# Leaving the softmax weights of eight heads unnormalised until the output projection loads them

## The chip, the cores and the metric

The kernel runs on one core of a Trainium2 chip, float32 in and out. The metric is the device time of one execution in microseconds (us), the median of several. PE is the matrix engine, PEld its weight loads, DVE the vector engine, ACT the scalar engine, POOL GpSimd, SP the engine whose queue issues all DMAs of this kernel.

## The reference, cut

Two layers of an encoder with 1024 tokens of width 1024. Each layer projects the normalised input, runs four groups of four heads, projects their 1024 concatenated outputs with `w_out`, adds a residual, and ends in a gated MLP. The groups are A (2-D neighbourhood), B (low-rank, "latent"), C (grouped-query) and D (sliding window). Only B and C are touched; both are dense attention:

```python
sc = jnp.einsum('bqhgd,bkhd->bhgqk', q_blk, k).astype(jnp.float32) * scale
p = jax.nn.softmax(sc, axis=-1).astype(v.dtype)
return jnp.einsum('bhgqk,bkhd->bqhgd', p, v)
...
mixed = jnp.concatenate([o_a, o_b, o_c, o_d], axis=-1) @ w_out[l]   # shapes left out
```

## The kernel before

Every fp32 matmul is made of rounded halves: an operand is split into a high part (a cast to the rounded type, on ACT or DVE) and a low part (the difference, on DVE or POOL).

Per layer the mixer runs sixteen heads in the order d0 to d3, c0 to c3, b0 to b3, a0 to a3, and of each head four pairs of 128-query tiles; one pair is a slot. `score` (L1030) works a slot: two score tiles of 128x1024 for a head of c or b (L1028), the negated row maximum on DVE (L1086), the exponential on ACT with the row sum as a by-product (L1105), the reciprocal of the sum on DVE (L1129), and for c and b the multiplication of the whole 128x1024 tile `P` by it on DVE (L1131). `gather` (L1142) then transposes the weights in chunks of four 128x128 blocks (L1183), casts the high half from PSUM on ACT (`PTh`, L1188), subtracts for the low half on DVE (`PTl`, L1193), multiplies both with the values on PE into `ob_mix` (L1210), adds the two halves of the result (`bot`, L1245) and stores it to DRAM in `oT` (L1249), transposed: 64 rows of a head by 1024 tokens. `PTh` and `PTl` take turns in a ring of five buffers (tag `PT`, `NPT` = 5).

The output projection runs a group behind, in the gaps: `out_group` (L771) loads two heads' rows of `oT` for half of the tokens at a time (L800, into a free part of `bias`), casts the high half on DVE (L801), makes the low half on POOL (L802), multiplies by `w_out` on PE (`pb_mix`, `od`, `oc`, `ob` with `wod`, `woc`, `wob`) and adds into `y` on DVE (L828). Group d is projected while c and b run, c while b and a run, b while a runs.

Each step is put at a time by a table `P` of numbers; a scheduler then orders every engine's instructions from those, their operands and the free buffers. Each engine and the SP queue work their instructions in that order, and an instruction that waits holds all behind it. Group a also loads many small pieces through SP: `va` (L895) and `za` (L865, L870).

Of the kernel before, what the change touches and what calls it, by code (L numbers as in the profile page):

```python
# [10 lines left out]
F32 = mybir.dt.float32  # L11
F32R = mybir.dt.float32r
AF = mybir.ActivationFunctionType
ALU = mybir.AluOpType
# [5 lines left out]
S = 1024  # L20
# [24 lines left out]
def r32(ap):  # L45
    return ap.bitcast(F32)
# [25 lines left out]
NP, NPT = 6, 5  # L72


class Kernel:
# [16 lines left out]
    def setup(self):  # L92
        nc, tc, ctx = self.nc, self.tc, self.ctx
        cp = self.cp = ctx.enter_context(tc.tile_pool(name="const", bufs=1))
        dr = self.dr = ctx.enter_context(tc.tile_pool(name="dram", bufs=1, space=DRAM))
        self.wp = ctx.enter_context(tc.tile_pool(name="wp", bufs=1))
        self.sm = ctx.enter_context(tc.tile_pool(name="small", bufs=8))
        self.big = ctx.enter_context(tc.tile_pool(name="big", bufs=1))
        self.psp = None
        self.banks_for("mix0")  # L100

        self.mhalf = cp.tile([128, 1], F32, name="mhalf", tag="mhalf")
        nc.vector.memset(self.mhalf, -0.5)
        self.eps = cp.tile([128, 1], F32, name="eps", tag="eps")
        nc.vector.memset(self.eps, EPS)
        self.z = dr.tile([NPIECE, 128, NT, 128], F32, name="z", tag="z")
        self.oT = dr.tile([D, S], F32, name="oT", tag="oT")
        self.gate = dr.tile([NFF, 128, S], F32, name="gate", tag="gate")
        self.xs = [dr.tile([S, D], F32, name=f"xs{i}", tag=f"xs{i}") for i in range(2 * DEPTH - 1)]


        self.gcol = cp.tile([128, DEPTH, NK], F32, name="gcol", tag="gcol")
        self.idf = cp.tile([128, 128], F32, name="idf", tag="idf")
        self.idr = cp.tile([128, 128], F32R, name="idr", tag="idr")
# [655 lines left out]
    def out_group(self, l, kind):  # L770

        nc = self.nc
        ov = self.oT.rearrange("(g k p) s -> g p k s", p=128, k=2)
        g = "abcd".index(kind)
        tag = f"{kind}{l}"
        ws = {}

        def begin():
            assert all(self.ow.get((kind, i)) == 4 for i in range(2 if kind == "a" else 4))
            if kind == "d":  # L780
                self.y = [self.share(i, F32, f"y{l}_{i}", (4, S)) for i in range(2)]
            if kind == "a":

                ws["x"] = [[self.reg["K"][:, e, :] for e in range(2)], self.o1]
            else:
                if kind == "d":
                    self.o = self.share(2, F32R, f"o{l}", (2, 2, S))
                ws["x"] = [(self.o[:, k, 0], self.o[:, k, 1]) for k in range(2)]

        def load(c):  # L790

            if c == 0:
                begin()
            assert kind in "ad" or all(("bcd"["bcd".index(kind) + 1], "mm", 4 * c + t) in self.ow for t in range(4))
            cols = slice(c * 512, c * 512 + 512)
            for k, (hi, lo) in enumerate(ws["x"]):
                if kind == "a" and k == 1:
                    break
                raw = self.bias[:, 3, (c if kind == "a" else k) * 512:][:, :512]
                nc.sync.dma_start(raw, ov[g, :, k, cols])  # L800
                nc.vector.tensor_copy(hi[:, cols], raw)  # L801
                nc.gpsimd.tensor_tensor(out=lo[:, cols], in0=raw, in1=r32(hi[:, cols]), op=ALU.subtract)  # L802

        def raw():
            ws["raw"] = [self.raw_weights([self.w_out[l][:, i * 512:(i + 1) * 512]], 2 * g, 2, f"wo{tag}_{i}")
                         for i in range(2)]

        def split():
            ws["w"] = [self.split_weights(x, f"wo{tag}_{i}") for i, x in enumerate(ws["raw"])]

        def mm(t, i):
            self.ow[kind, "mm", t] = 1
            bank = None if i else "pb"
            ws["ps", t, i] = ps = self.ps1([128, 512], F32, f"o{tag}") if bank is None else self.half(bank, True)
            if kind == "a":
                assert self.ow[kind, 2] == 4 and (kind, 3, t // 4 * 2 + 1) in self.ow
            with self.begin(bank):
                last = self.mm3(ps, [([x[:, t * 128:(t + 1) * 128] for x in ws["x"][k]], [x[:, k, :] for x in ws["w"][i]])
                                     for k in range(2)])
            self.through(bank, last)  # L820

        def add(t, i):
            ps = ws["ps", t, i]
            y = self.y[t // 4][:, t % 4, i * 512:(i + 1) * 512]
            if kind == "d":
                nc.scalar.copy(y, ps)
            else:
                nc.vector.tensor_tensor(out=y, in0=y, in1=ps, op=ALU.add)  # L828

        return dict(load=load, raw=raw, split=split, mm=mm, add=add)  # L830

    def slot(self, kind, n):
# [198 lines left out]

    def score(self, hd, pair, t0, ln):

        nc, kind, i = self.nc, hd["kind"], hd["i"]
        st = hd[pair] = dict(P={})
        tag = f"{hd['tag']}_{pair}"

        def tile(j, t):
            qt = 2 * pair + j
            x = {}  # L1040
# [5 lines left out]
            else:  # L1046

                r0, e = 8 * (pair // 2) + 4 * j, pair % 2
# [62 lines left out]
            def norm():  # L1111
                st["ok"] = j + 1
                if kind in "da" and j == 0:
                    return
                rr = st["rr"][:, j:j + 1]
                if kind == "d":

                    nc.vector.tensor_tensor(out=st["sum"], in0=st["sum"], in1=st["es"], op=ALU.add)
                    nc.vector.reciprocal(st["rr"], st["sum"])
                    if st["pd"][0].shape == x["p"].shape:  # L1120
                        both = st["p"].rearrange("p (a b) -> p a b", b=512)[:, :, :n]
                        todo = [(both, st["rr"].unsqueeze(2).to_broadcast([128, 2, n]))]
                    else:
                        todo = [(p, st["rr"][:, e:e + 1].to_broadcast(list(p.shape))) for e, p in st["pd"].items()]
                elif kind == "a":
                    nc.vector.reciprocal(st["rr"], st["sum"])
                    todo = [(p, st["rr"][:, e:e + 1].to_broadcast(list(p.shape))) for e, p in st["pd"].items()]
                else:
                    nc.vector.reciprocal(rr, st["sum"][:, j:j + 1])  # L1129
                if kind in "bc":  # L1130
                    nc.vector.tensor_scalar(out=x["p"], in0=x["p"], scalar1=rr, scalar2=None, op0=ALU.mult)  # L1131
                    return
                for p, r in todo:
                    nc.gpsimd.tensor_tensor(out=p, in0=p, in1=r, op=ALU.mult)
# [3 lines left out]
            self.at(t + d, top)  # L1138
            self.at(t + d + n / 1000 + P["EXP"], exp)
            self.at(t + d + n / 500 + P["EXP"] + P["NRM"], norm)  # L1140

        tile(0, t0 + P[f"S{kind.upper()}0"] * ln)  # L1142
# [666 lines left out]
```

## Time and profile before

| | us |
|---|---|
| median of three runs | 2690.39 (2689.8 to 2691.87) |
| the profiled execution, its own time | 2694.25 |
| its span, first to last instruction | 2692.4 |
| PE busy in the span | 2565.2 |
| DVE busy | 2111.1 |
| ACT busy | 1463.6 |

The first layer's heads of c and b lie at about 290 to 558 us of the span, its heads of a at 558 to 640, and what turns `y` into the MLP's operands up to 720. The second layer repeats this from 1622. Idle time of an engine is put to what released it; a releaser written `DVE P_b L1131` is the last DVE instruction of that line before the wait ended. PE's ends are modelled, so a busy PE can still stand between two matmuls; its waits show better on PEld, which must load the weights first.

### The profile page before, as it was taken

How to read it: one execution, taken by the hardware profiler on the slowest of the kernel's cores; microseconds unless marked ns; L12 is line 12 of the kernel's file. 1: busy time of each engine (PE TensorE's matmuls, PEld its weight loads, DVE VectorE, ACT ScalarE, POOL GpSimd, SP SyncE). 2: the span in 40 equal slices, each digit the busy share in tenths (PEclk: the TensorE clock that was granted, in tenths of full speed). 3: DMA queues.
4: the chain of work that ended last, by engine and by line, in shares of the span. 5: the costliest groups of instructions: out<-in, count | busy, mean ns of one | idle time of the engine just before them, and what ended most of it. 6: DMA issues, size and time to landing. Idle time of an engine off the chain costs nothing. (4 is left out here: it accounts for less than half of the span.)

```text
span 2692.4 us, 40234 instructions
## 1 busy us (share of the span) xinstructions
PE 2565.2 (95%) x14533; PEld 2210.0 (82%) x14533; DVE 2111.1 (78%) x3099; ACT 1463.6 (54%) x2704; POOL 798.2 (30%) x761
## 2 busy tenths in 40 slices
PE   7999999997799999999999999999968999999998
PEld 7999888885688888788789998888757888888886
DVE  5347899989878888878854568999797778888787
ACT  5347677666544444544653466776664444454433
POOL 1343212264333343100234432112743333330001
PEclk9999999999899999999999999999988999999999
DMA  6343412234222222550352434122432222226502
GB/s 190 106 131 91 107 49 68 56 72 152 76 90 77 94 79 79 188 203 17 97 163 86 124 96 94 50 71 55 113 126 79 71 95 71 86 71 227 179 1 102
DMA packets 316913, 268.00 MB, mean 100 GB/s; under 512 B 104762, under 2 KB 262570, under 8 KB 316714
## 3 DMA queue, kind: packets, MB, share of 16 engines
q1 hardware_dynamic: 316714, 265.43, 32.9%
q8 instruction: 114, 1.87, 0.3%
q14 instruction: 85, 0.70, 0.1%
HBM read 183.30 MB, written 69.48 MB: 94 GB/s over the span
## 5 line engine op out<-in xcount | busy, mean ns | idle before, releaser
L1309 POOL TENSOR_TENSOR sums<-loads 128x512 f32<-128x512 f32 x84 | 170.0, 2023 | 153.0 <-DMA loads<-in_w_up 67.2
L1309 POOL TENSOR_TENSOR loads<-loads,sums 128x512 f32<-128x512 f32 x42 | 57.7, 1374 | 372.4 <-DVE wgl L1319 229.5
L1530 ACT CAST dhP<-rows 128x1024 fp32r<-128x1024 f32 x88 | 89.4, 1052 | 130.1 <-issue 53.7
L86 POOL TENSOR_TENSOR rs_pf<-rs_pf,mhalf 128x1 f32<-128x1 f32 x15 | 13.9, 928 | 467.7 <-ACT rs_pf L85 467.6
L1531 DVE TENSOR_TENSOR dlP<-rows,dhP 128x1024 fp32r<-128x1024 f32 x88 | 105.2, 1219 | 40.7 <-ACT dhP L1530 40.7
L255 PE MATMUL dx<-dhP 128*128 128x512 f32 x308 | 120.2, 390 | 1.1 <-DVE yfQ L1597 1.1
L257 PE MATMUL dx<-dhP,dlP 128*128 128x512 f32 x308 | 120.0, 389 | 0.0
L256 PE MATMUL dx<-dlP,dhP 128*128 128x512 f32 x308 | 119.8, 389 | 0.0
L1188 ACT CAST PTh_b<-pt_b 128x512 fp32r<-128x512 f32 x128 | 74.9, 587 | 57.6 <-PE pt_b L1183 56.5
L257 PE MATMUL ux<-fT,wql 128*128 128x512 f32 (+1 forms) x272 | 102.6, 377 | 0.0
L255 PE MATMUL pb_mix<-whi_wa,h 128*128 128x256 f32 x320 | 100.0, 313 | 0.1
L1376 ACT ACTIVATE c<-ug,cw 128x1024 f32<-128x1024 f32 x44 | 54.7, 1244 | 82.4 <-DMA gate<-c 79.4
L255 PE MATMUL ux<-fT,wqh 128*128 128x512 f32 (+1 forms) x256 | 96.9, 378 | 1.4 <-ACT fT L275 1.4
L1377 DVE SCALAR_TENSOR_TENSOR c<-ug,cw,c 128x1023 f32<-128x1023 f32 x44 | 56.8, 1291 | 51.4 <-ACT c L1376 51.4
L256 PE MATMUL ux<-fT,wqh 128*128 128x512 f32 (+1 forms) x256 | 96.5, 377 | 0.0
L1419 ACT ACTIVATE c<-c 128x1024 f32<-128x1024 f32 x44 | 46.7, 1062 | 85.7 <-DVE c L1379 85.7
L1193 DVE TENSOR_TENSOR PTl_c<-pt_c,PTh_c 128x512 fp32r<-128x512 f32 x128 | 85.5, 682 | 8.5 <-ACT PTh_c L1188 7.9
L1188 ACT CAST PTh_c<-pt_c 128x512 fp32r<-128x512 f32 x128 | 74.5, 587 | 32.4 <-PE pt_c L1183 30.6
L1193 DVE TENSOR_TENSOR PTl_b<-pt_b,PTh_b 128x512 fp32r<-128x512 f32 x128 | 87.0, 683 | 6.3 <-ACT PTh_b L1188 5.4
L1028 PE MATMUL s_b<-rK,rQ 128*128 128x512 f32 x256 | 91.5, 414 | 0.4 <-ACT P_b L1105 0.4
L257 PE MATMUL pb_mix<-whi_wa,h 128*128 128x256 f32 x320 | 90.3, 282 | 0.0
L256 PE MATMUL pb_mix<-wlo_wa,h 128*128 128x256 f32 x320 | 90.3, 282 | 0.0
(681 smaller groups left out, 9710.5 us busy)
## 6 DMA issues: line engine op xcount, KB each, us to landing
loads<-in_w_up SPq DMA_DIRECT2D x84, 512.0 KB
gate<-c SPq DMA_DIRECT2D x44, 512.0 KB
z<-z SPq DMA_DIRECT2D x28, 512.0 KB
rows<-gate SPq DMA_DIRECT2D x56, 256.0 KB
rows<-in_w_down SPq DMA_DIRECT2D x56, 256.0 KB
rK<-rK SPq DMA_DIRECT2D x48, 256.0 KB
xs<-xo SPq DMA_DIRECT2D x16, 512.0 KB
xf<-xs SPq DMA_DIRECT2D x16, 512.0 KB
```

The lines of the kernel that those rows point to most:

```text
L255: nc.tensor.matmul(out, ah, bh, start=start and i == 0, stop=False, **flags)
L256: nc.tensor.matmul(out, ah, bl, start=False, stop=False, **flags)
L257: last = nc.tensor.matmul(out, al, bh, start=False, stop=stop and i == n - 1, **flags)
L1028: nc.tensor.matmul(out[:, c:c + w], Q[:, qt * 128:(qt + 1) * 128], K[:, k0 + c:k0 + c + w], start=i == 0, stop=i == len(ops) - 1)
L1188: nc.scalar.copy(x["sp"][0][:np, :n], x["pt"][:np, :n])
L1193: nc.vector.tensor_tensor(out=x["sp"][1][:np, :n], in0=x["pt"][:np, :n], in1=r32(x["sp"][0][:np, :n]), op=ALU.subtract)
L1309: nc.gpsimd.tensor_tensor(out=out, in0=a, in1=b, op=op)
L1376: nc.scalar.activation(c, u, AF.Identity, bias=b, scale=w1)
L1377: nc.vector.scalar_tensor_tensor(out=c[:, 1:], in0=u[:, :S - 1], scalar=w0, in1=c[:, 1:], op0=ALU.mult, op1=ALU.add)
L1419: nc.scalar.activation(a, a, AF.Gelu_apprx_tanh)
L1530: nc.scalar.copy(hi, src)
L1531: nc.vector.tensor_tensor(out=lo, in0=src, in1=r32(hi), op=ALU.subtract)
```

## The change

The 128 multiplications of L1131 go. After the second tile of a slot the two reciprocals of each of 128 rows, `rr`, are stored by one DMA to a new DRAM tile `rsum` of 8 heads by 1024 tokens. When `out_group` loads rows of b or c, it takes a further buffer `r` from the ring `PT`, fills it with two DMAs (for each of two heads one row of 512 sums, repeated over 64 partitions), and multiplies the raw rows by it on DVE before the split. The transposes now take the weights as the exponential leaves them.

```diff
+        self.rsum = dr.tile([8, S], F32, name="rsum", tag="rsum")
...
                 nc.sync.dma_start(raw, ov[g, :, k, cols])
+                if kind in "bc":
+                    r = self.ap.tile([128, 512], F32, tag="PT", name=f"r{tag}_{c}_{k}", bufs=NPT)
+                    for e in range(2):
+                        nc.sync.dma_start(r[64 * e:64 * e + 64], self.rsum["bc".index(kind) * 4 + 2 * k + e, cols]
+                                          .partition_broadcast(64))
+                    nc.vector.tensor_tensor(out=raw, in0=raw, in1=r, op=ALU.mult)
                 nc.vector.tensor_copy(hi[:, cols], raw)
...
                 if kind in "bc":
-                    nc.vector.tensor_scalar(out=x["p"], in0=x["p"], scalar1=rr, scalar2=None, op0=ALU.mult)
+                    if j == 1:
+                        nc.sync.dma_start(self.rsum["bc".index(kind) * 4 + i, pair * 256:pair * 256 + 256]
+                                          .rearrange("(j p) -> p j", p=128), st["rr"])
                     return
```

The scheduler orders the engines anew. In the changed program the lines below L802 are 7 to 10 higher. On DVE, where group c's last slot (`c0_3_3`: layer 0, head 3, pair 3) meets b's first, before:

```order
L1129 RECIPROCAL rr_b0_0_0_5431<-sum_b0_0_0_5429 128x1
L801 CAST o0_4176<-bias0_4172 128x512
L1131 TENSOR_SCALAR P_b0_0_0_0_5433<-P_b0_0_0_0_5433,rr_b0_0_0_5431 128x1024
L1193 TENSOR_TENSOR PTl_c0_3_3_2_5483<-pt_c0_3_3_2_5477,PTh_c0_3_3_2_5482 128x512
L1129 RECIPROCAL rr_b0_0_0_5431<-sum_b0_0_0_5429 128x1
L1131 TENSOR_SCALAR P_b0_0_0_1_5461<-P_b0_0_0_1_5461,rr_b0_0_0_5431 128x1024
L1193 TENSOR_TENSOR PTl_c0_3_3_3_5510<-pt_c0_3_3_3_5504,PTh_c0_3_3_3_5509 128x512
L1086 TENSOR_REDUCE nm_b0_0_1_5533<-s_b0_0_1_0_5537 128x1
L1193 TENSOR_TENSOR PTl_b0_0_0_0_5531<-pt_b0_0_0_0_5525,PTh_b0_0_0_0_5530 128x512
```

and after, on the same engine at the same place:

```order
L1137 RECIPROCAL rr_b0_0_0_5416<-sum_b0_0_0_5414 128x1
L1203 TENSOR_TENSOR PTl_c0_3_3_2_5468<-pt_c0_3_3_2_5462,PTh_c0_3_3_2_5467 128x512
L1137 RECIPROCAL rr_b0_0_0_5416<-sum_b0_0_0_5414 128x1
L1203 TENSOR_TENSOR PTl_c0_3_3_3_5494<-pt_c0_3_3_3_5488,PTh_c0_3_3_3_5493 128x512
L1203 TENSOR_TENSOR PTl_b0_0_0_0_5515<-pt_b0_0_0_0_5509,PTh_b0_0_0_0_5514 128x512
L1094 TENSOR_REDUCE nm_b0_0_1_5517<-s_b0_0_1_0_5521 128x1
```

The two multiplications are gone, and the cast of `o` that stood between has moved to a later place, behind its new product.

On the SP queue, where group b's second half of rows is loaded during the heads of a (`va0_2` are pieces of head a2's values, `oT<-bot` result stores), before:

```order
L1249 DMA oT_81<-bot_a0_0_2_7580 64x8x32
L895 DMA va0_2_7629<-z_80 40x2x64 x23
L1249 DMA oT_81<-bot_a0_0_3_7678 64x8x32
L800 DMA bias0_4172<-oT_81 128x512
L1249 DMA oT_81<-bot_a0_1_0_7760 64x8x32
```

and after:

```order
L1259 DMA oT_81<-bot_a0_0_2_7573 64x8x32
L902 DMA va0_2_7622<-z_80 40x2x64 x24
L1259 DMA oT_81<-bot_a0_0_3_7671 64x8x32
L801 DMA bias0_4169<-oT_81 128x512
L805 DMA rb0_1_0_7701<-rsum_82 64x512 x2
L801 DMA bias0_4169<-oT_81 128x512
L805 DMA rb0_1_1_7708<-rsum_82 64x512 x2
L1259 DMA oT_81<-bot_a0_1_0_7761 64x8x32
```

The four loads of sums stand behind the 24 small loads, and the second raw load stands here too.

On DVE, around the first low half of the second pair of head a1 (`PTl_a0_1_1_0`), before:

```order
L1193 TENSOR_TENSOR PTl_a0_1_0_1_7699<-pt_a0_1_0_1_7694,PTh_a0_1_0_1_7698 120x384
L1126 RECIPROCAL rr_a0_1_2_7657<-sum_a0_1_2_7655 128x2
L1096 ISA P_a0_1_3_0_7748,nm_a0_1_3_7743<-s_a0_1_3_0_7747,bi0_1_7378 128x440
L1096 ISA nm_a0_1_3_7743 128x1
L1193 TENSOR_TENSOR PTl_a0_1_1_0_7742<-pt_a0_1_1_0_7736,PTh_a0_1_1_0_7741 120x512
L1245 TENSOR_TENSOR bot_a0_1_0_7760<-ob_mix0_73,bot_a0_1_0_7760 64x256
```

and after:

```order
L1104 ISA P_a0_2_2_0_7990,nm_a0_2_2_7985<-s_a0_2_2_0_7989,bi0_2_7720 128x440
L1104 ISA nm_a0_2_2_7985 128x1
L1104 ISA P_a0_2_2_0_7990,nm_a0_2_2_7985<-s_a0_2_2_0_7989,bias0_4169 128x320
L1104 ISA nm_a0_2_2_7985 128x1
L807 TENSOR_TENSOR bias0_4169<-bias0_4169,rb0_1_0_7701 128x512
L1203 TENSOR_TENSOR PTl_a0_1_1_0_7743<-pt_a0_1_1_0_7737,PTh_a0_1_1_0_7742 120x512
L808 CAST o0_4173<-bias0_4169 128x512
```

The chunk of head a1 now stands behind the product with the sums, and behind the score bias of head a2's pairs 0 to 2, which the kernel before had later.

## Rows read from the trace of the kernel before

**Rows 1.** The page's first part: busy time, share of the span, instructions.

```profile
PE 2565.2 (95%) x14533; PEld 2210.0 (82%) x14533; DVE 2111.1 (78%) x3099; ACT 1463.6 (54%) x2704; POOL 798.2 (30%) x761
```

**Rows 2.** Busy time by stage: window, its length, each engine, PE clock, DMA.

```profile
core 0: us, PE busy (x) PEld busy (x) DVE busy (x) ACT busy (x) POOL busy (x), PEclk, DMA share, GB/s
290.00:558.00 268.00, 264.25 (x1766) 230.23 (x1766) 248.51 (x432) 195.99 (x369) 60.39 (x61) 1.00 0.27 65
558.00:640.00 82.00, 75.79 (x462) 63.12 (x463) 68.70 (x158) 50.77 (x121) 50.77 (x68) 1.00 0.39 104
640.00:720.00 80.00, 56.89 (x353) 47.99 (x352) 71.24 (x93) 43.95 (x87) 20.91 (x21) 0.87 0.31 106
1622.00:1892.00 270.00, 265.53 (x1773) 231.16 (x1773) 250.23 (x435) 197.21 (x371) 60.91 (x61) 1.00 0.27 65
```

**Rows 3.** Instruction groups on DVE: line, shapes, count | busy us, mean ns | idle before.

```profile
L1131 DVE TENSOR_SCALAR P_c<-P_c,rr_c 128x1024 f32<-128x1024 f32 x64 | 52.1, 816 | 0.5
L1131 DVE TENSOR_SCALAR P_b<-P_b,rr_b 128x1024 f32<-128x1024 f32 x64 | 50.8, 793 | 0.7
...
L757 DVE TENSOR_TENSOR y<-y 128x512 f32<-128x512 f32 x32 | 20.4, 683 | 0.0
...
L1434 DVE TENSOR_TENSOR c<-c,c 128x1024 f32<-128x1024 f32 x44 | 85.6, 1946 | 1.1
```

**Rows 4.** Waits of PEld, 290 to 560 us: us in total, times, longest.

```profile
PEld ob_mix L1210 <- DVE PTl_b L1193: 2.2, 5, 1.2
PEld pt_c L1183 <- ACT rQ L1001: 1.8, 6, 0.4
PEld pt_b L1183 <- DVE P_b L1131: 1.7, 3, 1.3
PEld ob_mix L1210 <- DVE PTl_c L1193: 1.1, 3, 0.7
PEld pt_c L1183 <- DVE P_c L1131: 1.1, 2, 0.9
PEld pt_b L1183 <- ACT rK L1001: 1.0, 4, 0.3
```

**Rows 5.** Line 1131 in the whole execution: who waited for it.

```profile
  PEld pt_b L1183: 3.4, 6
  PEld pt_c L1183: 2.3, 4
```

**Rows 6.** Waits of ACT, 290 to 560 us, for the row maxima.

```profile
ACT P_b L1105 <- DVE nm_b L1086: 4.3, 8, 1.5
...
ACT P_c L1105 <- DVE nm_c L1086: 2.3, 5, 0.6
```

**Rows 7.** SP's issues by line: ns min/median/max of one; then its longest waits, 290 to 700.

```profile
L1249 SPq DMA_DIRECT2D oT<-bot_b x32: 445/468/613, 429.7 to 1896.4; - x32
L931 SPq DMA_DIRECT2D rK<-rK x24: 579/596/646, 187.6 to 1924.8; - x24
SPq L1249 <- DVE bot_c L1245: 46.9, 10, 8.0
SPq L1249 <- DVE bot_b L1245: 27.0, 10, 7.8
```

**Rows 8.** Timeline, start and us: a raw load's issue on SP, its cast on DVE.

```profile
280.97 0.34 SPq L800 DMA_DIRECT2D bias<-oT  x1
283.75 0.43 DVE L801 CAST o<-bias 128x512 fp32r<-128x512 f32 x1 [1.89 <-DMA bias<-oT]
```

**Rows 9.** Timeline of SP, then of DVE, during the heads of a.

```profile
573.31 0.62 SPq L1249 DMA_DIRECT2D oT<-bot_a  x1
573.99 9.13 SPq L895 DMA_DIRECT2D va<-z  x23
583.23 0.62 SPq L1249 DMA_DIRECT2D oT<-bot_a  x1
583.90 0.63 SPq L800 DMA_DIRECT2D bias<-oT  x1
...
580.40 0.69 DVE L1193 TENSOR_TENSOR PTl_a<-pt_a,PTh_a 120x512 fp32r<-120x512 f32 x1
```

## The prediction

> **What bounds the kernel now.** The page's first part says PE is busy 95% of the span, DVE 78% [rows 1], so the question is how far PE stands still where the change acts. The view by stage answers for the heads of c and b: of 268 us PE is busy 264.25 and DVE 248.51, that is 98.6% and 93% [rows 2]. The second layer is alike: 265.53 and 250.23 of 270. PE bounds this stage, and DVE is so full that PE often meets an operand that DVE has not finished. How much that costs is in the waits of PEld, the view to trust where PE's ends are modelled [rows 4]: the waits of 290 to 560 us add up to some 17 us, none longer than 1.3. I sort them by what PE waited for. For the normalised weights: 1.7 and 1.1, together 2.8. For the low halves that DVE makes: 2.2 and 1.1 and three smaller ones of 1.2 together, in all 4.5. For copies and exponentials of ACT: 1.8, 1.0 and nine smaller ones of 4.5 together, in all 7.3. After 558 us the picture turns: in the heads of a PE is busy 75.79 of 82 and DVE 68.70, and then, to 720 us, PE only 56.89 of 80 and DVE 71.24, at a granted PE clock of 0.87 [rows 2]. There DVE is close to the bound.
>
> **The change part by part.**
>
> *The removed multiplications.* DVE loses 52.1 + 50.8 = 102.9 us [rows 3], all inside the stages of c and b. This is off the path: PE is the engine that ends the stage. What the span can gain is PE's waits.
>
> (1) Transposes wait for the exponential instead of the product. The waits for L1131 vanish: 2.8 us in layer 0, and 3.4 + 2.3 = 5.7 in both layers [rows 5].
>
> (2) DVE's queue gets shorter. In layer 0 its work falls from 248.5 to about 248.5 - 51.4 + 2.7 = 200 us, 75% of 268 (51.4 is half of 102.9; 2.7 is (4), below). A low half then waits less behind other DVE work. The waits in question are 0.2 to 1.2 us, the product that stood ahead of them takes 0.8 [rows 3, 4]. So I take half of 4.5, 2.25 us a layer; bounds 0 and 4.5.
>
> (3) ACT waits 4.3 + 2.3 = 6.6 us for row maxima that DVE is late with [rows 6], and the copies behind those exponentials are among what PE waits for. I take a third of 7.3, 2.4 us a layer; bounds 0 and 7.3.
>
> Together 2.8 + 2.25 + 2.4 = 7.45 a layer, 15 us in both. What is late next is PE itself.
>
> *The added products.* (4) Per layer 8 products of 128x512, 16 in all. The nearest row is another sum of two SBUF operands of that shape, 683 ns [rows 3]: 10.9 us of DVE. The four of group c fall to the heads of b, where DVE has just lost far more: nothing, with that slack as cover. The four of group b fall to the heads of a, with DVE at 84% and nearly full after: I charge them in full, 4 x 0.683 = 2.7 a layer, 5.4 us in both. Bounds: 0, if DVE's 13 idle us of that stage take them, and a stretched product. For that the rows give 1946 ns for 1024 elements [rows 3], 973 for 512, so 7.8 us. The Trainium skill ("SBUF", section "Who interferes with whom") says that a DVE instruction with two SBUF inputs contends with a GpSimd instruction that reads SBUF; the stage of a is where POOL is busiest, 50.77 of 82 us [rows 2], so by this rule the term is nearer 7.8, by the short row 5.4. I stay with 683 ns since both kinds of row exist and half of POOL's work there is short.
>
> *The stores of sums.* (5) 32 DMAs a layer of 128x2 values. No row shows 256 runs of four bytes. The nearest issues take 0.47 us (64 runs) and 0.6 (64 runs of an on-chip copy) [rows 7]: 15 to 19 us of SP a layer, 0 if SP only waits then. In that stage SP waits 46.9 + 27.0 us for `bot` alone [rows 7], so I take 0. Behind each store on SP stand result stores, swaps of K and loads of z; it waits for the reciprocal of its own slot, which comes before the result that the next store waits for anyway. The cover is that wait; without it 19 us of SP a layer would come before the K that PE needs. The store also keeps `rr` longer, but the next writer of that buffer comes two slots later, about 17 us.
>
> (6) *The loads of sums.* Eight DMAs a layer and group, 0.596 us each by the nearest row [rows 7]: 4.8 us of SP. For c they stand among waits: 0. A load needs about 2.8 us from issue to use (280.97 to 283.75, a whole 256 KB) [rows 8]. In the new DVE order the first product of c stands six instructions behind the reciprocal that frees the queue for them, some 4.3 us of work, so I take no wait there; bound 2.8 a layer. For b they stand behind 24 small loads; I take 0, bound 4.8 a layer of SP's time in a stage in which SP works almost without a gap [rows 9]. The worse course is rival C.
>
> (7) *The ring.* `r` holds two of five `PT` buffers for some 3 to 5 us, four times a layer. A chunk takes two buffers, so one and a half chunks stay in flight. I take 0 because the order puts other matmuls there; the cost without that cover is one wait of about 2.8 us each, 11 a layer, the upper end of C.
>
> The sum: -15 + 5.4 = -9.6 us. Against the profiled execution that is 2694.25 - 9.6 = 2684.7 (its span 2692.4 to 2682.8); the median of the runs lies 3.9 us under that execution, so the forecast is 2690.4 - 9.6 = **2681 us**. Its own range, with (2) to (4) at milder values, is 2673 to 2688.
>
> **The rivals.**
>
> *A, DVE was the brake of the whole stage.* If all of PE's waits for DVE and ACT vanish, the gain is 2 x (2.8 + 4.5 + 7.3) = 29.2, and 29.2 - 5.4 = 23.8 remain: 2667. For it: DVE at 93%. Against it: ACT is busy only 196 of 268 us, so many of its late copies come from the fixed order rather than from DVE.
>
> *B, hidden anyway.* Only the direct waits go, 5.7, and the products cost 5.4: 2690. For it: PE is busy 98.6% of the stage, and each wait removed can reappear at the next in-order operand, which in the new order is the exponential on ACT.
>
> *C, the small transfers stall the heads of a.* On SP the loads of sums stand behind 24 loads that take 9.13 us for 23, 0.4 each though they move 20 KB each [rows 9]. In the trace they end at 583.12; two result and raw issues follow to 584.53, then two loads of sums of 0.6 (584.5 to 585.7), the second landing 2.8 after its issue began, at 587.9, and the product, 588.6. The low half of head a1 that stands behind this product ran at 580.40 [rows 9]. That is 8.2 us a layer, 16.4 in both: 2690.4 - 15 + 5.4 + 16.4 = 2697, slower. It decides once DVE reaches the product before 587.9. Against it: the new order gives DVE, between the result of head a0's third pair and the product, eleven score biases, three low halves, six additions and more, some 16 us, whereas SP needs about 15. That is close. The Trainium skill ("DMA: Bandwidth & Descriptors", section "Rules for kernel authors") speaks against the change here: it says to coalesce many small transfers, as one under 64 KB is mostly overhead. The trace agrees, with 0.4 us of queue for 20 KB [rows 9] and 0.34 for 256 KB [rows 8].
>
> **How the numbers follow.** Forecast 0.44, A 0.14, B 0.22, C 0.20. The likeliest gives 2681. The range is 2660 to 2700: below it is A with free products (2661), above it C with the ring's waits. About 0.2% (5.4 us) is what a measurement of this kernel can tell from no change. Faster by more than that is under 2685: A and most of the forecast, 0.55. Within: B and the forecast's upper edge, 0.25. Slower, over 2695.8: C, 0.20.
>
> **What would show it.** In the changed profile no transposes wait for a DVE multiplication; DVE is busy about 200 us of the stage of c and b; PEld's waits for low halves halve, and those for ACT shrink by a third; the stage shortens by 5 to 9 us a layer. The heads of a and what follows to the MLP take as long as before, plus up to 3. C would show as DVE or PEld waiting for a DMA `rb<-rsum` or its product, B as new waits of transposes for the exponential. The forecast is wrong if the stage of c and b keeps its 268 us, or if more than 3 us a layer come back between 558 and 720.

## The result

| | before | after |
|---|---|---|
| median of the runs (us) | 2691.13 (2689.8 to 2692.05) | 2819.51 (2816.09 to 2823.49) |
| ratio, 95% interval | | 1.0478 (1.046 to 1.0496) |
| the profiled execution, its span | 2694.25, 2692.4 | 2818.06, 2816.1 |

The change costs 128.4 us, where 10 were forecast as a gain. The page of the changed kernel answers to [rows 1], its windows to [rows 2]:

```profile
span 2816.1 us, 40448 instructions
...
PE 2612.5 (93%) x14533; PEld 2242.1 (80%) x14533; DVE 2052.5 (73%) x2987; ACT 1467.0 (52%) x2704; POOL 794.0 (28%) x761
```

```profile
290.00:558.00 268.00, 234.77 (x1481) 204.03 (x1481) 176.85 (x302) 165.40 (x304) 41.62 (x36) 0.93 0.41 57
558.00:640.00 82.00, 71.98 (x443) 60.39 (x441) 60.84 (x124) 47.56 (x101) 34.39 (x55) 0.96 0.35 66
...
1622.00:1892.00 270.00, 242.66 (x1667) 218.07 (x1666) 181.92 (x370) 173.85 (x359) 57.85 (x51) 0.94 0.48 73
```

In the same 268 us PE does 1481 matmuls instead of 1766, stands still for 33 us instead of 4, and its granted clock falls from 1.00, the upper of its two levels (2.4 GHz; the lower is 1.2), to a mean of 0.93. Over the whole execution PE is busy 47 us longer for the same 14533 matmuls ([rows 1]); how much of the loss is this slower work behind the stalls, and how much the stalls themselves, no run separates. DVE has become idle, as wanted, and nobody profits. The DMA engines are busier, 0.41 for 0.27, and move less, 57 GB/s for 65: the first sign of the cause.

How late each group of heads ends in layer 0 shows in the issues of the result stores of b and of the first two heads of a (ns min/median/max of one, first and last start), of before, then of after:

```profile
L1249 SPq DMA_DIRECT2D oT<-bot_b x16: 445/468/613, 429.7 to 562.5; - x16
L1249 SPq DMA_DIRECT2D oT<-bot_a x8: 580/620/625, 565.8 to 601.9; - x8
```

```profile
L1259 SPq DMA_DIRECT2D oT<-bot_b x16: 445/478/1907, 445.9 to 609.5; - x16
L1259 SPq DMA_DIRECT2D oT<-bot_a x8: 615/620/636, 615.2 to 665.9; - x8
```

Group b ends 47 us late and these heads of a 64 us late. The second layer repeats it: there the last of these stores of a is issued at 2059.7 us instead of 1935.8, 124 us late.

What PEld, DVE and SP wait for in the changed kernel, 290 to 640 us (in total, times, longest), is of a new kind. In [rows 4] no wait exceeds 1.3 us:

```profile
PEld ob_mix L1220 <- DVE bot_b L1255: 17.6, 4, 7.2
PEld pb_mix L256 <- DVE o L808: 8.1, 2, 8.0
PEld ob_mix L1220 <- DVE PTl_c L1203: 6.7, 3, 6.3
PEld s_c L1035 <- issue: 4.5, 1, 4.5
...
DVE bias L807 <- DMA rc<-rsum: 17.0, 3, 8.3
...
ACT bot_b L1240 <- DMA oT<-bot_b: 10.6, 2, 8.6
ACT P_a L1113 <- DMA rsum<-rr_b: 7.4, 1, 7.4
...
PE s_c L1035 <- DMA rK<-rK: 4.3, 1, 4.3
...
SPq L902 <- DMA rsum<-rr_b: 18.3, 4, 5.7
...
SPq L801 <- DMA oT<-bot_d: 10.8, 1, 10.8
```

These are a few long stalls. Eight stops of PEld are longer than 2 us, and the seven of them over 3 us can be followed back to a DMA that landed late: one to the raw load of group d, three to loads of sums (`rc<-rsum`), one to a swap of K, one to a result store that still held its buffer `bot_b`, and one to a store of sums, for which an exponential of a waited 7.4 us. One in full, on SP's timeline of the changed kernel (start, us), then on DVE and PEld:

```profile
291.79 0.38 SPq L1140 DMA_DIRECT2D rsum<-rr_c  x1
292.21 0.47 SPq L1021 DMA_DIRECT2D bias<-rpb  x1
292.78 0.45 SPq L1259 DMA_DIRECT2D oT<-bot_d  x1
293.33 0.53 SPq L342 DMA_DIRECT2D z<-sta  x1
293.95 0.44 SPq L850 DMA_DIRECT2D z<-z  x1
305.23 0.33 SPq L801 DMA_DIRECT2D bias<-oT  x1
...
307.94 0.43 DVE L808 CAST o<-bias 128x512 fp32r<-128x512 f32 x1 [8.02 <-DMA bias<-oT]
...
309.02 0.50 PEld L1220 LDWEIGHTS ob_mix<-PTl_c,rV 128*128 128x128 f32 x2 [6.26 <-DVE PTl_c L1203]
```

Before, the same two steps follow each other at once:

```profile
292.72 0.45 SPq L1249 DMA_DIRECT2D oT<-bot_d  x1
293.27 0.53 SPq L341 DMA_DIRECT2D z<-sta  x1
293.90 0.44 SPq L843 DMA_DIRECT2D z<-z  x1
294.67 0.33 SPq L800 DMA_DIRECT2D bias<-oT  x1
```

The raw load must wait until the result store has landed. Before, the raw load follows 2 us after the issue of that store; behind a store of sums it follows after 12. DVE stands 8 us at the cast, the low half behind the cast is late, and PE behind that. The store of sums itself took SP only 0.38 us.

### The profile page after: what moved, and what is told of

Same layout as the page of the kernel before. It is cut to its first block, busy times and chain, and to the rows that moved or that the text cites. A ratio compares the mean times of both kernels' runs of the same rounds, so it can differ in the third digit from the quotient of the medians.

```text
span 2816.1 us, 40448 instructions
## 1 busy us (share of the span) xinstructions
PE 2612.5 (93%) x14533; PEld 2242.1 (80%) x14533; DVE 2052.5 (73%) x2987; ACT 1467.0 (52%) x2704; POOL 794.0 (28%) x761
## 5 line engine op out<-in xcount | busy, mean ns | idle before, releaser
L256 PE MATMUL pb_mix<-whi_wa,h 128*128 128x256 f32 x320 | 101.1, 316 | 0.1
L1035 PE MATMUL s_c<-rK,rQ 128*128 128x512 f32 x256 | 83.4, 430 | 10.8 <-DMA rK<-rK 10.8
L1094 DVE TENSOR_REDUCE nm_c<-s_c 128x1 f32<-128x1024 f32 x64 | 77.8, 1216 | 21.2 <-PE s_c L1035 21.0
L1113 ACT ACTIVATE P_c<-s_c,nm_c 128x1024 f32<-128x1024 f32 x64 | 71.7, 1121 | 38.5 <-DVE nm_c L1094 38.4
```

The source lines that it names most:

```text
L256: nc.tensor.matmul(out, ah, bh, start=start and i == 0, stop=False, **flags)
L1035: nc.tensor.matmul(out[:, c:c + w], Q[:, qt * 128:(qt + 1) * 128], K[:, k0 + c:k0 + c + w], start=i == 0, stop=i == len(ops) - 1)
L1094: nc.vector.tensor_reduce(nm, x["s"], axis=AX.X, op=ALU.max, negate=True)
L1113: nc.scalar.activation(x["p"], x["s"] if kind in "bc" else x["p"], AF.Exp, bias=st["nm"][:, j:j + 1], scale=1.0 if kind in "bc" else -1.0, ...
```

## The experiments

Each difference below is to the kernel before, run beside it (medians 2687.9 to 2691.1). By the intervals of the ratios each is known to some 3 to 5 us.

| what is in the kernel | us | to before |
|---|---|---|
| normalisation gone, nothing added | 2689.19 | -1.8 |
| ... and products | 2695.17 | +5.5 |
| ... and loads into the ring | 2719.64 | +28.7 |
| ... and stores: the change | 2819.51 | +128.4 |
| before, with the stores | 2754.84 | +63.9 |

The first theory held that the stores cost it all (S), its rivals the loads (L) or the new rhythm without the normalisation (N).

**Stores alone.** In the kernel before:

```diff
                     nc.vector.tensor_scalar(out=x["p"], in0=x["p"], scalar1=rr, ...)
+                    if j == 1:
+                        nc.sync.dma_start(self.rsum[...].rearrange("(j p) -> p j", p=128), st["rr"])
```

> The kernel before, which keeps its normalisation of the weights, with the 64 stores of reciprocals added on SP's queue and nothing that reads them. Theory S (the stores are the cost: 256 runs of four bytes land late and hold up whatever is issued behind them): most of the 128 us between the two kernels appear, 2770 to 2830. Theory L (the loads of sums are the cost: two of five PT buffers held and SP stopped until they are free): 2690 to 2700. Theory N (the removal itself hurts, because PE, ACT and DVE meet in another rhythm): 2690 to 2700.

It took 2754.84, 1.0237 (1.022 to 1.0254). The stores alone, at 1 us each, cost half of the whole; S gave too much, L and N are wrong by 55 us.

**Everything but the stores.**

```diff
-                    if j == 1:
-                        nc.sync.dma_start(self.rsum[...], st["rr"])
...
+        nc.sync.dma_start(self.rsum.rearrange("a (b c) -> (a b) c", c=64), one)
```

> The changed kernel without its 64 stores of reciprocals; the rows in DRAM are filled with ones once at the start, so the loads, the ring and the products are all there but the weights of these heads stay unnormalised in the result. Theory S: the time falls to 2675 to 2695, about the prediction. Theory L: it stays at 2790 to 2830, and DVE still waits for the loads of sums. Theory N: 2790 to 2830 too, with no wait for a load.

2719.64, 1.0105 (1.009 to 1.012): 100 us are gone with the stores, but S expected 2695 at most; loads and products are not free either. The stores thus cost 64 us in the old order and 100 in the new one.

**Normalisation gone, nothing in its place.**

```diff
-                    nc.vector.tensor_scalar(out=x["p"], in0=x["p"], scalar1=rr, ...)
```

> The kernel before with the 128 normalising multiplications taken out and nothing put in their place, so the result leaves the normalisation of these heads out. It measures the gain that the prediction put at 15 us (5.7 to 29): S and L both expect 2675 (2661 to 2685). Theory N expects 2790 or more.

2689.19, 0.9991 (0.9981 to 1.0001), a gain between 5.1 us and none. N falls, and so does the 15 us gain. The stage of c and b, and PEld's waits from 290 to 560 us:

```profile
290.00:558.00 268.00, 266.12 (x1774) 233.22 (x1773) 211.93 (x370) 196.12 (x369) 58.21 (x61) 0.99 0.26 65
...
PEld pt_c L1183 <- DVE PTl_c L1193: 2.4, 5, 1.3
...
PEld ob_mix L1210 <- DVE PTl_b L1193: 0.9, 4, 0.3
```

Two of the three kinds of wait shrink as forecast: none is left for a product, and those for ACT fall from 7.3 us to 4.7. Those for low halves do not: all rows of them add up to 5.1 before and 5.6 now, 0.9 instead of 2.2 at `ob_mix` for `PTl_b`, but 2.4 instead of 0.7 at `pt_c` for `PTl_c`. In all 12.8 us of waits are left of 16.7. And PE was busy 264.25 us of 268 and is busy 266.12 now. By this view PE had 3.75 us to win, not 7.45; that most of those weight loads waited while matmuls already queued kept PE busy fits it, but is not shown.

Still group b ends earlier, and the gain is lost behind it. The last result store of b and the first store behind the heads of a, of the residual stream (`xs<-xo`), without the normalisation:

```profile
L1249 SPq DMA_DIRECT2D oT<-bot_b x16: 451/469/612, 429.7 to 555.6; - x16
L310 SPq DMA_DIRECT2D xs<-xo x8: 319/323/338, 639.7 to 677.1; - x8
```

and that second store before (the first is shown above, to 562.5):

```profile
L310 SPq DMA_DIRECT2D xs<-xo x8: 319/323/338, 639.8 to 677.2; - x8
```

The 6.9 us at the end of b are 0.1 at the end of the heads of a. From 290 to 558 us PE does only 8 matmuls more (above), which speaks for another order of its work rather than for more of it. In the second layer 8.6 us (1887.8 against 1896.4) shrink to 2.0 (1973.4 against 1975.4).

**Stores issued by ACT** instead of SP, else the changed kernel.

```diff
-                        nc.sync.dma_start(self.rsum[...], st["rr"])
+                        nc.scalar.dma_start(self.rsum[...], st["rr"])
```

> The changed kernel with its stores of reciprocals issued by ACT instead of SP. If the stores hurt because they stand in SP's order (SP waits for a reciprocal while swaps of K and loads of z stand behind it, or the queue works in order), most of the loss goes: 2690 to 2740, with some loss at ACT, which now waits for a reciprocal 32 times a layer. If they hurt in the DMA engines that all queues share, it stays at 2790 or more. Under theory L too it stays at 2790 or more.

2838.37, 1.0549 (1.0533 to 1.0564). Another queue doesn't help. At the place shown above the raw load still waits for the result store, 9.7 us now (ACT's queue, then SP's):

```profile
291.15 0.39 ACTq L1140 DMA_DIRECT2D rsum<-rr_c  x1
...
292.49 0.45 SPq L1259 DMA_DIRECT2D oT<-bot_d  x1
...
302.15 0.33 SPq L801 DMA_DIRECT2D bias<-oT  x1
```

So the place of the stores in SP's order isn't what delays it. What is left is behind the queues, in something that both share; which part, no run shows. (ACT waits for the reciprocals here, so the 19 us more are no measure of that.)

**Runs of eight bytes.** Each partition's two values lie side by side in DRAM.

```diff
-                                          .rearrange("(j p) -> p j", p=128), st["rr"])
+                                          .rearrange("(p j) -> p j", j=2), st["rr"])
```

> The changed kernel whose stores lie in DRAM so that each partition writes its two values next to each other: 128 runs of eight bytes instead of 256 of four, the same 64 stores at the same places (so rows are divided by the sums of other rows). The stores cost the changed kernel about 100 us (2819.5 against 2719.6 without them). Theory R (the cost goes by the number of runs): about half of it goes, 2760 to 2780. Theory D (it goes by the number of DMAs put into SP's queue): it stays at 2810 to 2825.

2727.12, 1.0139 (1.0122 to 1.0156): the stores now cost 8.8 us instead of 100. Both theories are wrong: half as many runs cost a tenth. Either the size of a run decides or a number of runs per DMA between 128 and 256. Two runs tell these apart.

**One column a store:** 128 runs of four bytes in each of 128 DMAs.

```diff
-                    if j == 1:
-                        nc.sync.dma_start(self.rsum[..., pair * 256:pair * 256 + 256]..., st["rr"])
+                    nc.sync.dma_start(self.rsum[..., qt * 128:qt * 128 + 128]..., rr)
```

> The changed kernel, each reciprocal column stored as soon as it is there: 128 stores of 128 runs of four bytes instead of 64 of 256. The stores of four bytes cost 100 us, those with 128 runs of eight bytes only 7.5 (2727.1 against 2719.6). Theory Z (it is the size: a run of four bytes is dear, one of eight is not): the 16384 runs of four bytes are all still there, 2800 to 2840. Theory K (it is the number of runs in one DMA, 256 against 128): 2725 to 2745, the extra being 64 more issues on SP.

**Each value twice:** 256 runs of eight bytes in each of 64 DMAs.

```diff
+                    nc.vector.reciprocal(st["r4"][:, 2 * j:2 * j + 2], st["sum"][:, j:j + 1].to_broadcast([128, 2]))
...
+                                          .rearrange("(j p x) -> p j x", p=128, x=2), ...)
```

> The changed kernel with every reciprocal written twice side by side, so a store is 256 runs of eight bytes at the same 64 places (the loads then read rows that belong to other tokens). Theory Z (size): 2722 to 2740, like the stores with 128 runs of eight bytes. Theory K (number of runs in one DMA): 2800 to 2830.

One column: 2859.49, 1.0639 (1.0617 to 1.066), 43 us more than the change and above Z's range (2840). Why the 64 further DMAs cost that much is open; ACT's exponentials of a wait 42.1 us for stores of `rr_b` in this run, 12.7 in the changed kernel, over the whole execution. Each value twice: 2728.61, 1.0146 (1.013 to 1.0161). The size of a run decides (Z): K is wrong both times, and Z's range only in the first. The pages of the changed kernel and of the one with each value twice, with the same number of packets:

```profile
q1 hardware_dynamic: 336682, 269.70, 36.1%
```

```profile
q1 hardware_dynamic: 336682, 269.77, 33.5%
```

With four bytes the packets hold each of the 16 engines for 0.361 x 2816.1 = 1017 us, with eight for 0.335 x 2729.1 = 914. At the place shown above the kernel with each value twice issues its raw load sooner, though still later than before:

```profile
293.06 0.45 SPq L1262 DMA_DIRECT2D oT<-bot_d  x1
...
298.92 0.33 SPq L801 DMA_DIRECT2D bias<-oT  x1
```

**Is it the write into DRAM?** The same runs as reads, and as writes into SBUF, both in the kernel before:

```diff
+                        nc.sync.dma_start(ld, self.rsum[...].rearrange("(j p) -> p j", p=128))
```

> The kernel before with 64 reads added where the stores of reciprocals stand: 256 runs of four bytes each, out of a DRAM tensor of ones into a small tile that nobody reads. The same runs as stores cost 64 us there (2754.8 against 2691.0). Theory M (writing a run of four bytes into DRAM is what is dear, and it holds up the other transfers): 2689 to 2698. Theory F (any run of four bytes is dear): 2735 to 2765.

```diff
+                        nc.sync.dma_start(ld[:, :, 0:1], st["rr"].unsqueeze(2))
```

> The kernel before with the 64 stores of reciprocals sent into a small SBUF tile instead of DRAM, as 256 runs of four bytes each, at the same places and with the same wait for the reciprocal. Theory M (DRAM's side of the write): 2689 to 2700. Theory F (any run of four bytes, or the wait of SP for the reciprocal with what stands behind it): 2740 to 2765.

Reads: 2704.0, 1.0052 (1.0034 to 1.007), +13.0, a little above what M expected. But this run is no equal of the stores. The reads wait for nothing, and the scheduler put all 64 of them, of both layers, ahead of the first heads of c:

```profile
L1138 SPq DMA_DIRECT2D ld_c<-rsum x32: 359/468/1587, 74.7 to 117.9; - x32
L1138 SPq DMA_DIRECT2D ld_b<-rsum x32: 359/421/495, 89.3 to 130.1; - x32
```

What reads cost among the result stores of c and b, no run shows. Into SBUF: 2699.64, 1.0038 (1.0023 to 1.0053), +8.7. These stand where the stores stand, from 292.5 to 1886.4 us, so against 63.9 for the same runs written to DRAM most of the cost comes with DRAM as the target. The packets' time on the pages fits M for the reads too, wherever they stand: 886 us for each DMA engine before (0.329 of the span), 958 with stores to DRAM (0.348), 892 into SBUF and 893 with the reads (0.330). The stage of c and b with stores to DRAM, then to SBUF:

```profile
290.00:558.00 268.00, 250.95 (x1637) 218.08 (x1636) 231.51 (x394) 180.86 (x333) 50.26 (x43) 0.97 0.36 59
```

```profile
290.00:558.00 268.00, 264.97 (x1774) 231.32 (x1774) 250.00 (x434) 197.00 (x372) 60.79 (x61) 1.00 0.29 65
```

The second, which has the same 64 issues on SP and the same wait for the reciprocal, bounds what the prediction took as the whole cost of a store: 8.7 us.

**Loads that wait for no store.** All stores stay, but the loads read ones.

```diff
-                        nc.sync.dma_start(r[64 * e:64 * e + 64], self.rsum[...]
+                        nc.sync.dma_start(r[64 * e:64 * e + 64], self.ones[...]
```

> The changed kernel with all its stores, but the loads read a second DRAM tensor that holds ones from the start, so no product waits for a store (and the weights of these heads stay unnormalised). With the normalisation kept, the stores cost 64 us; after the change they cost 100. Theory W (the other 36 us are DVE, PE behind it, waiting for loads that wait for the last stores to land): 2775 to 2790. Theory R without W (the changed order alone exposes more of the same delays): 2810 to 2820.

2797.15, 1.0395 (1.0378 to 1.0412), between the two: +107.5 against +128.4. Of the 36 us by which the stores cost more in the new order, some 21 hang on the loads' waiting for the stores. DVE's waits for the loads of c over the whole execution, in the changed kernel, then here:

```profile
DVE bias L807 <- DMA rc<-rsum: 27.9, 5, 8.3
```

```profile
DVE bias L811 <- DMA rc<-ones: 15.5, 5, 5.6
```

Without stores there is no such wait at all. So the loads land late even where they wait for no store. The other 15 us come with the new order, and which waits they are stays open.

**Sums transposed once a head,** stored as 8 runs of 512 bytes:

```diff
+                nc.tensor.transpose(pt[:8, 0, :], hd["rrh"], self.idf)
+                nc.scalar.copy(rT[:8], pt[:8, 0, :])
+                nc.sync.dma_start(self.rsum[...].rearrange("(q p) -> q p", p=128), rT[:8])
```

> The changed kernel with the eight reciprocal columns of a head collected in one 128x8 tile, transposed by PE once a head, copied by ACT and stored as 8 runs of 512 bytes: 16 stores of 4 KB instead of 64 of 1 KB, 128 runs instead of 16384. Theories R and D: the cost of the stores is gone, 2718 to 2735, which is the kernel without stores (2719.6) plus 16 transposes and copies. If it is any wait for a store that lands just before its use: 2740 to 2780. None expects it under 2691.

2733.16, 1.016 (1.0145 to 1.0175), +43.5: 15 us above the kernel without stores, no better than eight bytes.

**The products alone,** then **the ring without loads** (the product writes into a buffer of `PT`), then **the loads without the ring** (4 columns of sums, 16 bytes a partition, into a small tile, so these loads are smaller too):

```diff
+                    nc.vector.tensor_tensor(out=raw, in0=raw, in1=raw, op=ALU.mult)
```

> Neither stores nor loads of sums: the 16 products are there, but multiply the block by itself, so they take DVE the same time and the result leaves the normalisation out. Loads and products together cost 30 us (2719.6 against 2689.2). Theory P (the products, in a stage in which DVE is nearly full, move the order of the work behind them): 2710 to 2720. Theory Q (the loads: SP's time and two of five PT buffers): 2687 to 2698.

```diff
+                    r = self.ap.tile([128, 512], F32, tag="PT", name=f"r{tag}_{c}_{k}", bufs=NPT)
+                    nc.vector.tensor_tensor(out=r, in0=raw, in1=raw, op=ALU.mult)
+                    raw = r
```

> Neither stores nor loads of sums: the 16 products multiply a block by itself and write into a buffer of the ring PT, from which the halves are then made, so the ring gives up a buffer as in the change but no DMA fills it (the normalisation is left out). The products alone give 2695.2, products with loads into the ring 2719.6. Theory G (the ring: chunks of the heads of a find no buffer and the scheduler puts them later): 2708 to 2722. Theory T (the loads: SP's time and their landing): 2693 to 2702.

```diff
-                    r = self.ap.tile([128, 512], F32, tag="PT", name=f"r{tag}_{c}_{k}", bufs=NPT)
+                    r = self.stat(4, f"r{tag}_{c}_{k}")
```

> The changed kernel without stores (rows of ones in DRAM from the start), whose 32 loads of sums stand where they stood but fill a small tile of 4 columns outside the ring, which the product then repeats along the row (the normalisation is left out). Theory G (the ring): 2692 to 2702. Theory T (SP's time and the landing of the loads): 2708 to 2722.

2695.17 (ratio 1.0021, 1.0011 to 1.0031), 2706.05 (1.0063, 1.0048 to 1.0078; just under what G expected) and 2697.69 (1.0029, 1.0019 to 1.0039): +5.5, +18.1 and +9.8, against +28.7 with loads into the ring. So the products cost 7.3 us over the kernel without normalisation, the loads' own time some 4, and what remains, 19, is the ring or the size of the loads. The ring without any load costs 12.6 over the products, and with loads of full size moving out of the ring gives 23 back (2728.36 to 2705.57, the last two runs below), so it is the ring. The heads of a from 580 to 600 us, loads without the ring, then with it:

```profile
580.00:600.00 20.00, 18.73 (x118) 15.85 (x117) 14.99 (x40) 11.43 (x30) 10.49 (x19) 1.00 0.34 76
```

```profile
580.00:600.00 20.00, 16.68 (x73) 12.52 (x72) 13.66 (x40) 9.72 (x27) 11.50 (x17) 0.80 0.31 81
```

What happens there with the ring, on SP, DVE, ACT and PE in turn:

```profile
585.96 1.14 SPq L808 DMA_DIRECT2D rb<-rsum  x2
...
587.83 1.08 SPq L808 DMA_DIRECT2D rb<-rsum  x2
...
594.84 0.69 DVE L810 TENSOR_TENSOR bias<-bias,rb 128x512 f32<-128x512 f32 x1
...
594.31 0.59 ACT L1199 CAST PTh_a<-pt_a 120x512 fp32r<-120x512 f32 x1
...
590.54 0.67 PE L1083 MATMUL s_a<-rK,rQ 128*128 128x440 f32 x2 [0.76 <-DVE nm_a L1107]
591.92 1.10 PE L1083 MATMUL s_a<-rK,rQ 128*128 128x440 f32 x2 [0.72 <-DVE nm_a L1107]
593.49 0.90 PE L1083 MATMUL s_a<-rK,rQ 128*128 128x320 f32 x2 [0.46 <-DVE nm_a L1107]
```

Two ring buffers belong to `r` from 586 and 588 until the products at 594.8 and 597.4, over 9 us, not the 3 to 5 of step (7). From 580.3 to 594.3 ACT casts no chunk. The cast at 594.31 comes before the product has freed a buffer, right behind the exponential ahead of it, so here it waited for its place in ACT's order, which the scheduler made for a ring with fewer buffers. From 589 on PE is left with scores, each with a gap before it, and then the same scores take longer (0.67, then 1.10): the granted clock of this stretch is 0.80, between its two levels (1.2 and 2.4 GHz), after PE had stood between matmuls.

**Both faults mended.** Runs of eight bytes with the product reading the sums in the order in which they lie; then, besides, the sums loaded in halves into two buffers outside the ring:

```diff
+                    w = raw.rearrange("q (b j p) -> q b j p", j=2, p=128)
+                    nc.vector.tensor_tensor(out=w, in0=w, in1=r.rearrange("q (b p j) -> q b j p", j=2, p=128), op=ALU.mult)
```

> The changed kernel with runs of eight bytes (each partition's two values side by side in DRAM, as in the run at 2727.1) and a product that reads the loaded sums in the order in which they now lie, so it computes the whole function. The order of reading costs DVE nothing that is known: 2720 to 2732. If reading r with a stride of two stretches the products by half, 2726 to 2740.

```diff
+                        r = self.wp.tile([128, 256], F32, tag="stage", name=f"r{tag}_{c}_{k}_{b}", bufs=2)
```

> As the kernel with runs of eight bytes and the right order, but the sums are loaded in halves of 256 columns into two buffers that stand idle in this stage, outside the ring PT: 64 loads and 32 products of half the size. Theory G (holding a ring buffer from the issue of a load to its product was what the loads cost): 2697 to 2710, the products' 6 us and the 7.5 of the stores being left. If SP's time matters, with twice as many loads among the pieces of the heads of a: 2710 to 2730. Nobody expects it under 2688, since taking the normalisation out altogether gave 2689.2.

2728.36, 1.0139 (1.0124 to 1.0155), and 2705.57, 1.0046 (1.0028 to 1.0064). The second is the best form of the idea that was found, +14.6 us, somewhat less than the prices above add up to without the ring (8.8 for the stores, 7.3 for the products, some 4 for the loads, 1.8 back). It doesn't beat the kernel before, and a form that keeps this order of the work has no more to win than the removal alone gave, 1.8 us and at most 5.

## Why the prediction was wrong

**Steps (1) to (3), -15 us: measured -1.8.** Steps (1) and (3) were right on their waits, step (2) was not: the waits for low halves were to halve and stayed (5.1 and 5.6 us; my 4.5 left out two small rows). The sum was wrong all the more. I added up waits of PEld as if they were idle time of PE, though the row that I read first says that PE stood still for 268 - 264.25 = 3.75 us of the stage, and 4.47 in the second layer [rows 2]: 8.2 in both. And I took an earlier end of the stage for an earlier end of the kernel. Group b did end 6.9 and 8.6 us earlier, inside the 5 to 9 that the prediction named as its sign, but this came back in the heads of a, as its sign of being wrong has it (more than 3 us a layer). B's 5.7 is nearer than the forecast's 15. DVE's relief was overrated as well: 52.1 + 50.8 = 102.9 us of instructions went, but DVE's busy time fell only from 2111.1 to 2037.4, which fits neighbours that overlap: the other groups kept their durations (`PTl_b` 683 and 688 ns).

**Step (4), +5.4: measured +7.3.** Right in size. The products of b took 5.9 us, near the short row and not the 7.8 of the stretched one. That was partly luck. By the rule of the Trainium skill ("SBUF — State Buffer", section "Who interferes with whom") such a product contends with a POOL instruction that reads SBUF. The trace agrees, product by product: three of the sixteen began while POOL was in the middle of its subtraction (L809), and they lasted until 0.55 us after its end (0.92, 0.92 and 1.38 us); the others took 0.67 to 0.69. Where ACT issues the stores, six of the eight products of b met POOL, and the eight took 9.1 us. The group in the changed kernel (busy us, mean ns, idle before):

```profile
L807 DVE TENSOR_TENSOR bias<-bias,rb 128x512 f32<-128x512 f32 x8 | 5.9, 740 | 0.0
```

**Step (5), 0: measured 100.** This step failed, by what it left out. I priced a store by its issue on SP and found cover for it; that price was right, 0.38 us an issue, and with its wait at most 8.7 in all. I named the 256 runs of four bytes, found that no row shows them, took the nearest rows of the issue, and never bounded the transfer: how late it lands and what it does to others in flight. The only bound, 19 us a layer, was of SP's time; an effect on other DMAs was put at nothing, without a reason. The word on `rr` failed too: I had its buffer wanted again only 17 us later, and exponentials of a waited 12.7 us for such stores in all.

The Trainium skill ("DMA: Bandwidth & Descriptors", section "Specifications") puts all transfers below 512 bytes in one class, with a read-modify-write. It makes no difference between sizes in that class; the runs here do: four bytes cost 100 us, eight cost 8.8 to 12. The section "Why small descriptors are slow (HBM only)" of the same page of the Trainium skill exempts transfers from SBUF to SBUF; that agrees with 8.7 us against 63.9.

**Step (6), 0: measured some 4,** within its bound of 4.8 a layer. With the stores there, DVE also waits 17 us for the sums of c in the first layer, where the bound was 2.8; step (6) took no wait because it counted the work behind the reciprocal and nothing for a store that lands late.

**Step (7), 0: measured 19.** Its upper end, 11 a layer or 22 in both, was right. I saw that r takes two of five buffers and set it to nothing "because the order puts other matmuls there". It did, scores and projections, but the projections ran out, and each score had a gap before it.

**The rivals.** C named the right suspect, small transfers, and the wrong ones: loads of 20 KB and sums in the heads of a, not the stores. It put the loss in the heads of a, where the larger part, 47 of 64 us in the first layer, lies in c and b. The wait that it named there did not come: DVE stands 0.0 us before the products of b (above). What is lost in the heads of a without any store, 23 us against C's 16.4, is mostly the ring. B is what the removal alone gives. A has nothing for it.

**The range** failed with steps (5) and (7), with either alone: without any store the kernel takes 2719.64, outside it too. An operation of which no row existed was given a range of one engine's issue time.

## What to carry to other kernels

Before costing a removed wait, read how long the bounding engine stands idle in that stage: the sum of its waits for operands was several times more here (some 17 us against 3.75). Then ask whether the stages behind keep what the stage wins. A new transfer has three prices, its issue, its landing, and what it does to transfers behind it; if the trace shows no transfer with runs like its own, the last two are unknown and belong in the range. Look for single four-byte values stored to DRAM next to traffic that matters: two values side by side cost a tenth here. A tile taken from a ring of a busy stage is paid by the work that needs the buffers: 16 such tiles cost 13 to 23 us here, by three pairs of runs.

## What the runs showed of the hardware

Writing runs of four bytes to DRAM was dear out of proportion: 16384 of them cost 64 to 100 us, as many of eight bytes 12 us, as many of four bytes into SBUF 8.7. They move next to nothing, and the loss appears at other DMAs: a raw load that had followed 2 us after the result store it waits for followed after 12, and after 9.7 with the stores on ACT's queue. A DVE product of two SBUF operands that began while POOL was in the middle of such an instruction ended 0.55 us after it, up to 1.38 us long instead of 0.68. What reads of four bytes would cost in the same place, what in the memory or the DMA engines does this, and where between four and eight bytes it sets in, no run here shows.
